# Hybrid decoder trunk on one core: x is also loaded channel-major, and the first projections multiply it before it is normed

## The chip, the core and the metric

The kernel runs on one core of a Trainium2 chip. The core has a matrix engine (PE, its weight loads PEld), a vector engine (DVE), a scalar engine (ACT), a third elementwise engine (POOL) and a queue that issues most of the transfers (SP). Each engine takes its instructions in program order; they meet through semaphores only. The metric is the device time of one execution in microseconds (us). A KB here is 1024 bytes.

## What is computed

One decoder layer for 512 tokens of 1024 channels. Cut to what matters here:

```python
h = rmsnorm(x, g_pre)              # x * rsqrt(mean(x*x, -1) + 1e-6) * g_pre
u = h @ W_in                       # 1024 x 11352, split by columns into
(gq, gk, gv, ga, gz, dq, dk, dv, iq, ik, iw, dz, xq, xz, gates) = split_cols(u)
y_gla = gla_mixer(gq, gk, gv, ga, gz, ...)     # gated linear attention, 4 heads
y_dsa = dsa_mixer(dq, dk, dv, iq, ik, iw, dz)  # indexer picks keys, then attention
y_mem = cross_mixer(xq, xz, rmsnorm(mem, g_mem), w_mem_kv)
merged = (sigmoid(g0) * (y_gla @ w_gla_out) + sigmoid(g1) * (y_dsa @ w_dsa_out)
          + sigmoid(g2) * (y_mem @ w_x_out))
x = x + rmsnorm(merged @ W_o, g_post)
```

The norm's factor rsqrt(...) belongs to a token, g_pre to a channel. So h @ W is also (x * g_pre) @ W with each token's result multiplied by its factor.

## The kernel before

Each fp32 operand is held as two parts, a high one (ACT, `high`, line 95) and the rest (DVE, `low`, lines 99 and 101), and each product is three products: high by high, high by low, low by high (`mm3`, lines 108 to 110). The weights come in chunks of 128 columns by 1024 channels: SP loads a pair of chunks (1 MB, `wraw`, two buffers), ACT makes `whi`, DVE makes `wlo`, four buffers of each.

The work is a list of units, one per chunk: 24 matmuls of 512 (or 384, in `iq`) columns for channel-major results (`unit_t`), or 48 of 256 for token-major ones (`unit_n`, used by `dv` and `gv`). A unit fills one PSUM bank with the tag `mm`, of which there are two, so a unit starts when the results of the unit two places ahead of it have been read. Bank tags `at` (three), `tp` (two) and `ac` (one) serve the small products. The main loop goes through the units; each has four quarters, and side work hangs in slots behind a quarter (`at(name, slot, function)`; a slot number above 3 counts on into the next units). Weight splits come about two units ahead of their use (`need`). Whatever is written first goes first on each engine's queue: the order is that of the code.

The units before `gqk0.0` are `dv.0`, `dv.1` (values of the sparse attention), `pc` (one chunk that holds ik, ga and iw), `gv0.0`, `gv0.1` (first values of the linear attention), `iq0.0` to `iq1.1` (indexer queries). `pc` gives `alow` (the gate's low rank part and the indexer's weights), `ar` (the operand of the gate products `pla`) and `ikh`, `ikl` (indexer keys). From `alow` PE transposes the weights `iw` (`turn_iw`, tile `iwps`); four `pla` products, one per head (`gate_log`), go on through Abs, Exp, Ln and a running sum (`gate_ln`, `gate_sum`, tile `cum`) to the factors of the linear attention (`gla_exps`). `bias_rows` makes one small product `prel`. The scores (`score`, tile `pis`) begin in `gqk0.0`.

The opening before `dv`: x is loaded token-major in eight pieces; ACT squares them, DVE and POOL make the factor, DVE scales by it and by g_pre (which PE has spread over the partitions, tile `gps`), PE transposes the result in 32 steps of 128 x 128 (tile `xps`), ACT and DVE split it into `hh` and `hl`, which all later projections read. Tokens 0 to 255 go first, `dv.0` runs on them, then tokens 256 to 511.

Of the kernel before, what the change touches and what calls it, by code (L numbers as in the profile page):

```python
# [57 lines left out]
def trunk(ctx, tc, x, mem, w_in, w_c, w_kv, w_out, w_o, cols, g_pre, g_mem, g_post, w_up, rel, onehot, out):  # L58
# [134 lines left out]
    def unit_n(name, first, lhs, tiles, done):  # L193
# [3 lines left out]
        def quarter(q):  # L197
# [3 lines left out]
            if name[:2] == "dv":  # L201
                j, half = divmod(q, 2)
                co = o[0][:, 256 * j:256 * j + 256]
                wh, wl = chunks[first + half][3]
                for p in range(3):
                    for k in range(4):
                        ah, al = lhs(4 * half + k, tiles[j])
                        pe.matmul(co, al if p == 1 else ah, (wl if p == 2 else wh)[:, :, k],  # L208
                                  start=half + p + k == 0, stop=(half, p, k) == (1, 2, 3))
                return  # L210
# [819 lines left out]
    xts = [[k2("yh", f"x{tt}{i}") for i in range(2)] for tt in range(4)]  # L1030
    xns = [[k2("acc", f"xn{tt}{i}") for i in range(2)] for tt in range(4)]

    def load_x(tt):
        for i in range(2):
            sp.dma_start(xts[tt][i], x[128 * tt:128 * tt + 128, 512 * i:512 * i + 512])
# [152 lines left out]
```

## Time and profile before

| | |
|---|---|
| median of 3 runs | 839.51 us (838.93 to 840.6) |
| profiled execution, its own time | 840.41 us |
| its span in the profile | 838.7 us |
| PE busy in the span | 825.1 us, 98% |
| DVE, ACT busy | 471.6 us (56%), 329.1 us (39%) |
| moved by DMA | 86.93 MB, mean 104 GB/s |

The page gives averages over the whole span. The profile's other views cut it by time (stretches, timeline), by engine, and by what a waiting engine waited for. Instructions of one engine overlap a little at their edges, so the distance between starts tells what one costs in a row, and a busy PE is not a PE at full rate: the distance between starts tells that too.

### The profile page before, as it was taken

The page shows a single profiled execution, that of the slowest core. Times are in us where ns is not written, and L with a number is a line of the kernel's source. Part 1 is how long each engine was busy: PE and PEld are TensorE (multiplying, and loading weights), DVE is VectorE, ACT ScalarE, POOL GpSimd, SP SyncE. Part 2 cuts the span into 40 slices and gives each one's busy share as a digit, 9 for nine tenths or more (in the row PEclk, how much of TensorE's full clock was granted, in tenths as well). Part 3 has the DMA queues.
Part 4 walks back from the last instruction along what each step waited for, and adds up shares of the span by engine and source line. Part 5 has one row for each costly group of instructions (what it writes and reads, how often), then busy time and mean ns, then how long its engine had stood idle before and what let it go on. Part 6 is the DMA issues. An engine that isn't in the chain of part 4 may idle for free.

```text
span 838.7 us, 10810 instructions
## 1 busy us (share of the span) xinstructions
PE 825.1 (98%) x4340; PEld 707.8 (84%) x4340; DVE 471.6 (56%) x839; ACT 329.1 (39%) x597; POOL 51.8 (6%) x77
## 2 busy tenths in 40 slices
PE   7999999999999999999999999999999999999997
PEld 5898888989888888888887888889989898888885
DVE  5578667777676545546677543445645554343623
ACT  5585555353433223334444422434334343322320
POOL 2000101000000020031122000000000000000000
PEclk9999999999999999999999999999999999999999
DMA  7333115221222222223122124232223241226402
GB/s 234 117 113 127 50 51 189 89 101 51 101 96 105 101 82 95 84 104 115 50 82 95 51 101 167 103 107 101 101 101 127 75 151 60 92 100 223 154 1 100
DMA packets 17101, 86.93 MB, mean 104 GB/s; under 512 B 2097, under 2 KB 2609, under 8 KB 8474
## 3 DMA queue, kind: packets, MB, share of 16 engines
q1 hardware_dynamic: 16474, 85.18, 29.1%
q10 hardware_dynamic: 576, 1.05, 0.3%
q8 instruction: 34, 0.56, 0.3%
q14 instruction: 17, 0.14, 0.1%
HBM read 83.03 MB, written 4.74 MB: 105 GB/s over the span
## 4 chain that ended last, share of the span: by engine, by line
PE 93%; DVE 2%; ACT 1%; issue 1%; DMA 1%; POOL 0%; SPq 0%; DVEq 0%; POOLq 0%; ACTq 0%
PE out L110 5%; PE out L108 5%; PE out L109 5%; PE pfin L110 2%; PE pfin L108 2%; PE pfin L109 2%; PE tpp L698 1%; PE dv.0_227 L208 1%; DMA x<-x 1%; PE dv.1_319 L208 1%; PE xps L294 1%; PE pov L109 1%; PE pa L560 1%; PE pov L110 1%; DVE wlo L99 1%
## 5 line engine op out<-in xcount | busy, mean ns | idle before, releaser
L99 DVE TENSOR_TENSOR wlo<-wraw,whi 128x1024 fp32r<-128x1024 f32 x133 | 166.0, 1249 | 78.2 <-ACT whi L95 77.4
L95 ACT ACTIVATE whi<-wraw 128x1024 fp32r<-128x1024 f32 x133 | 138.7, 1052 | 22.0 <-PE out L109 19.8
L108 PE MATMUL out<-yh,whi 128*128 128x512 f32 x192 | 75.3, 392 | 0.0
L110 PE MATMUL out<-yh,wlo 128*128 128x512 f32 x192 | 74.8, 390 | 0.0
L109 PE MATMUL out<-yl,whi 128*128 128x512 f32 x192 | 74.8, 389 | 0.0
L684 ACT ACTIVATE bm<-bm,nm 128x128 f32<-128x128 f32 (+3 forms) x32 | 18.0, 564 | 76.5 <-DVE nm L682 76.5
L668 POOL TENSOR_TENSOR bm<-toe,madd 128x128 f32<-128x128 f32 (+3 forms) x32 | 31.5, 1003 | 195.9 <-DMA toe<-bd 125.8
L110 PEld LDWEIGHTS out<-yh,wlo 128*128 128x128 f32 x192 | 36.0, 188 | 7.6
L108 PEld LDWEIGHTS out<-yh,whi 128*128 128x128 f32 x192 | 36.1, 188 | 7.3
L109 PEld LDWEIGHTS out<-yl,whi 128*128 128x128 f32 x192 | 36.1, 188 | 7.2
L273 POOL TENSOR_TENSOR rstd<-var,mhalf 128x1 f32<-128x1 f32 x10 | 5.5, 554 | 388.1 <-DVE var L929 289.7
L95 ACT ACTIVATE yh<-th 128x512 fp32r<-128x512 f32 x16 | 10.1, 632 | 46.5 <-DVE th L632 27.6
L492 DVE SCALAR_TENSOR_TENSOR gth<-gth,out 128x512 f32<-128x512 f32 x16 | 11.0, 687 | 28.1 <-PE out L110 28.1
L433 DVE MATCH_REPLACE8 madd<-m,madd 128x256 f32<-128x256 f32 (+2 forms) x48 | 25.6, 543 | 0.0
L429 DVE MAX8 m<-madd 128x8 f32<-128x256 f32 (+2 forms) x48 | 23.6, 547 | 0.0
L682 DVE CUSTOM_DVE_ANT_0 bm<-lg,bm 128x128 f32<-128x128 f32 (+3 forms) x32 | 15.5, 486 | 12.8 <-PE lg L110 12.5
L728 DVE TENSOR_TENSOR ydsa<-pov,th 128x128 f32<-128x128 f32 x32 | 7.8, 285 | 22.3 <-PE pov L110 22.3
L95 ACT ACTIVATE pth<-tpp 128x128 fp32r<-128x128 f32 (+3 forms) x32 | 13.7, 428 | 12.7 <-PE tpp L698 12.6
L99 DVE TENSOR_TENSOR yl<-th,yh 128x512 fp32r<-128x512 f32 x16 | 11.1, 693 | 11.2 <-ACT yh L95 11.2
L419 DVE SCALAR_TENSOR_TENSOR madd<-relu,iw,madd 128x256 f32<-128x256 f32 (+2 forms) x21 | 12.9, 616 | 7.6 <-ACT relu L415 7.1
L926 ACT ACTIVATE sq<-pfin 128x512 f32<-128x512 f32 x8 | 4.8, 598 | 31.2 <-PE pfin L110 31.2
L99 DVE TENSOR_TENSOR ptl<-tpp,pth 128x128 fp32r<-128x128 f32 (+3 forms) x32 | 15.4, 483 | 0.0
(1026 smaller groups left out, 2357.2 us busy)
## 6 DMA issues: line engine op xcount, KB each, us to landing
wraw<-w_in SPq DMA_DIRECT2D x43, 1024.0 KB, 4.7
wraw<-w_out SPq DMA_DIRECT2D x12, 1024.0 KB, 4.7
wraw<-w_kv SPq DMA_DIRECT2D x8, 1024.0 KB, 4.7
wraw<-w_o SPq DMA_DIRECT2D x4, 1024.0 KB, 4.8
bd<-bs SPq DMA_DIRECT2D x1, 2560.0 KB
x<-x SPq DMA_DIRECT2D x8, 256.0 KB, 6.3
toe<-bd SPq DMA_DIRECT2D x8, 256.0 KB, 4.9
xres<-x SPq DMA_DIRECT2D x4, 512.0 KB, 8.0
```

The source lines that it names most:

```text
L95: act.activation(hi, src, AF.Copy, scale=scale)
L99: dve.tensor_tensor(lo, src, f(hi), op=OP.subtract)
L108: pe.matmul(o, lh, rh, start=first, stop=False)
L109: pe.matmul(o, lh, rl, start=False, stop=False)
L110: pe.matmul(o, ll, rh, start=False, stop=last)
L208: pe.matmul(co, al if p == 1 else ah, (wl if p == 2 else wh)[:, :, k], start=half + p + k == 0, stop=(half, p, k) == (1, 2, 3))
L419: dve.scalar_tensor_tensor(sc, r[:, :n], iw[:, b, h:h + 1], sc, op0=OP.mult, op1=OP.add)
L429: dve.max(out=M8[b], in_=maskadd[b])
L433: dve.match_replace(out=maskadd[b], in_to_replace=M8[b], in_values=maskadd[b], imm_value=-FMAX)
L668: pool.tensor_tensor(bm[:, :n], Q[hp]["toe"][i][:, 384 - 128 * qb:512], maskadd[qb], op=OP.add)
L682: dve.tensor_tensor_reduce(out=bm[:, :n], in0=lg[:, :n], in1=bm[:, :n], scale=-1.0, scalar=FMAX, op0=OP.add, op1=OP.min, accum_out=nm)
L684: act.activation(bm[:, :n], bm[:, :n], AF.Exp, scale=-1.0, bias=nm, accum_out=su)
```

## The change

x comes a second time, as `x_t`, channel-major (128 partitions, 8 channel groups of 512 tokens), loaded in four pieces `xt` between the two halves of the `dv` weights; the token-major x follows behind the `gv0` weights and serves for the squares alone. ACT and DVE split `xt` times g_pre into `gh`, `gl`. The units `dv`, `gv0`, `pc` and `iq0` multiply these, and their results are scaled by the token's factor: token-major ones by a column while they are split, channel-major ones by a row that PE spreads over the partitions (`rstd_row`, tile `rps`), in a multiplication on DVE (`pc_done`, `iq_done`). The normed `hh`, `hl` are made on DVE and ACT from `xt`, the column g_pre and that row (`h_norm`, one channel group per slot), for `iq1` and all later units. There are no transposes of x and no `gps`. Twelve products on zeros stand ahead of `dv`. `dv` runs as two halves over channels in four banks. `pc` moves behind `gv0`; what hangs on it (`gate_operands`, `turn_iw`, `gate_log`, `gate_ln`, `gate_sum`, `bias_rows`) moves by some units, and `col` is issued by ACT.

```diff
-    dvh, dvl = kv4("dvh", [4, 256], F32R), kv4("dvl", [4, 256], F32R)
-    def dv_done(i, p):
-        p3 = p.rearrange("p (t d) -> p t d", t=2)
-        split(dvh[:, 2 * i:2 * i + 2], dvl[:, 2 * i:2 * i + 2], p3)
-    win_n("dv", dv_done)
+    def dv_done(tt, p):
+        if tt == 0:
+            R["dvh"], R["dvl"] = kv4("dvh", [4, 256], F32R), kv4("dvl", [4, 256], F32R)
+        split(R["dvh"][:, tt], R["dvl"][:, tt], p[:, :256], R["rstd"][:, tt:tt + 1])
+    win_n("dv", None)
+    def dv_half(half, po):
+        wh, wl = chunks[half][3]
+        for p, ks in ((0, (0, 1)), (0, (2, 3)), (1, (0, 1, 2, 3)), (2, (0, 1, 2, 3))):
+            for k in ks:
+                for tt in range(4):
+                    ah, al = g_lhs(4 * half + k, tt)
+                    pe.matmul(po[tt][:, :256], al if p == 1 else ah, (wl if p == 2 else wh)[:, :, k],
+                              start=half + p + k == 0, stop=(half, p, k) == (1, 2, 3))
+    def rstd_row():
+        p = psum("tp", "rps")
+        for tt in range(4):
+            pe.matmul(p[:, 128 * tt:128 * tt + 128], R["rstd"][:, tt:tt + 1].to_broadcast([128, 128]),
+                      ident, start=True, stop=True)
+        R["row"] = w2("row")
+        act.activation(R["row"], p, AF.Copy)
+    def h_norm(k):
+        if k < KT:
+            xt = R["xt"][k // 2][:, k % 2]
+            dve.scalar_tensor_tensor(xt, xt, gpre[:, k:k + 1], R["row"], op0=OP.mult, op1=OP.mult)
+        if k:
+            split(hh[:, k - 1], hl[:, k - 1], R["xt"][(k - 1) // 2][:, (k - 1) % 2])
-    def pc_done(p):
+    def pc_done(o):
+        p = w2("pc")
+        dve.tensor_tensor(p, o, R["row"], op=OP.mult)
...
-    add_chunks(w_c, False, 1)
-    unit_t("pc", h_rhs, pc_done)
...
+        if h == 0:
+            for j in range(2):
+                tt = 2 * i + j
+                split(vh[:, tt], vl[:, tt], p[:, 256 * j:256 * j + 256], R["rstd"][:, tt:tt + 1])
+            return
...
-    win_n("gv0", lambda i, p: gv_done(0, i, p))
+    win_n("gv0", lambda i, p: gv_done(0, i, p), g_lhs)
+    add_chunks(w_c, False, 1)
+    unit_t("pc", g_rhs, pc_done)
...
-    at("gv0.0", 0, gate_operands)
-    at("gv0.0", 2, turn_iw)
-    for h in range(4):
-        at("gv0.1", h, gate_log, h)
+    at("gv0.0", 1, rstd_row)
+    for tt in range(4):
+        at("pc", tt // 2, lambda tt=tt: dv_done(tt, R["dvps"][tt]))
+    for k in range(9):
+        at("gv0.0", 3 + k, h_norm, k)
...
-    def iq_done(i, p):
+    def iq_done(u, i, o):
+        if u == 0:
+            p = w2("iqf", n=384)
+            dve.tensor_tensor(p, o[:, :384], R["row"][:, 128:512], op=OP.mult)
...
-    at("iq0.0", 2, gate_ln, 0)
-    at("iq0.0", 3, gate_ln, 1)
+    at("iq0.0", 0, gate_operands)
+    at("iq0.0", 2, turn_iw)
+    for h in range(4):
+        at("iq0.1", h, gate_log, h)
+    at("iq1.0", 0, gate_ln, 0)
+    at("iq1.0", 1, gate_ln, 1)
...
-        at("iq0.1", 1 + 4 * h, gate_sum, h)
+        at("iq1.0", 2 + 2 * h, gate_sum, h)
...
-    at("gv0.0", 1, bias_rows)
+    at("iq0.0", 3, bias_load)
+    at("iq1.1", 1, bias_rows)
...
-        load_x(0)
-        load_x(1)
-        load_next(2)
-        load_x(2)
-        load_x(3)
...
+        for half in range(2):
+            sp.dma_start(wdv[:, half], loads[0][0][:, half])
+            for k in (2 * half, 2 * half + 1):
+                sp.dma_start(R["xt"][k], x_t[:, 2 * k:2 * k + 2])
         load_next()
+        for tt in range(4):
+            sp.dma_start(xs[tt], x[128 * tt:128 * tt + 128])
...
+        idle = psum("ac", "idle")
+        for i in range(12):
+            pe.matmul(idle, zeros[:, 0:128], zeros, start=True, stop=True)
+        R["dvps"] = [psum(t, "dvps") for t in ("at", "at", "at", "ac")]
+        for half in range(2):
+            need(half, True)
+            for k in range(4 * half, 4 * half + 4):
+                gh.append(k2("yh", f"gh{k}", F32R))
+                gl.append(k2("acc", f"gl{k}", F32R))
+                split(gh[k], gl[k], R["xt"][k // 2][:, k % 2], gpre[:, k:k + 1])
+            dv_half(half, R["dvps"])
+        need(3, True)
+        ss, v = s8("ss", 4), s8("var", 4)
+        for tt in range(4):
+            act.activation(xs[tt], xs[tt], AF.Square, scale=1.0 / 32, accum_out=ss[:, tt:tt + 1])
...
+        dve.tensor_scalar(v, ss, EPS, None, op0=OP.add)
+        R["rstd"] = const.tile([128, 4], F32, name="rstd")
+        pool.tensor_tensor(R["rstd"], v, mhalf[:, :4], op=OP.pow)
```

The code's order decides what stands where on each queue. Three places follow. On DVE, from the results of `dv` to those of `pc`, before:

```order
L99 TENSOR_TENSOR dvl<-dv.1_319,dvh 128x512
L99 TENSOR_TENSOR wlo<-wraw,whi 128x1024
L99 TENSOR_TENSOR ikl<-pc,ikh 64x512
L99 TENSOR_TENSOR wlo<-wraw,whi 128x1024
L99 TENSOR_TENSOR ar<-alow,at__432 16x512
L99 TENSOR_TENSOR uph<-upraw,at__432 16x512
```

and the last third of the same stretch after, ahead of the multiplication of `pc` by the row:

```order
L101 SCALAR_TENSOR_TENSOR dvl<-dvps,rstd,dvh 128x256 x2
L330 SCALAR_TENSOR_TENSOR xt_114<-xt_114,col,row 128x512
L99 TENSOR_TENSOR hl<-xt_113,hh 128x512
L99 TENSOR_TENSOR wlo<-wraw,whi 128x1024
L330 SCALAR_TENSOR_TENSOR xt_114<-xt_114,col,row 128x512
L99 TENSOR_TENSOR hl<-xt_114,hh 128x512
L337 TENSOR_TENSOR pc<-pc,row 128x512
L99 TENSOR_TENSOR ikl<-pc,ikh 64x512
L99 TENSOR_TENSOR hl<-xt_114,hh 128x512
```

Between the `vl` of `gv0.0` and `pc<-pc,row` there now stand eight scalings of `xt`, seven `hl`, two `wlo`, two more `vl` and four `dvl`, where DVE had nothing of its own to do for `pc` but `ikl`. On PE, the transposes `iwps` before, inside `gv0.0`, with a quarter of `gv0.0` behind them:

```order
L108 MATMUL gv0.0_418<-whi,hh 128x256
L109 MATMUL gv0.0_418<-wlo,hh 128x256
L110 MATMUL gv0.0_418<-whi,hl 128x256
L338 MATMUL iwps<-ident,alow 128x64 x4
```

and after, inside `iq0.0`, with the first `pla` behind a quarter of `iq0.0` and one of `iq0.1`:

```order
L110 MATMUL iq0.0_518<-gh_236,wlo 128x384
L364 MATMUL iwps<-ident,alow 128x64 x4
L108 MATMUL iq0.0_518<-gh_240,whi 128x384
L109 MATMUL iq0.0_518<-gl_241,whi 128x384
L110 MATMUL iq0.0_518<-gh_240,wlo 128x384
```

`iwps` has moved from a place three quarters of a `gv` unit behind `pc` to one three quarters of an `iq` unit behind it, and `pla` with it. On ACT, from the first queries `iqe` on, before:

```order
L373 ACT_TABLE_LOAD
L373 ACTIVATE ebig<-ebig 128x1024
L95 ACTIVATE iqe<-iq0.0_576 64x384
L95 ACTIVATE iqo<-iq0.0_576 64x384
L373 ACTIVATE ebig<-ebig 128x1024
L95 ACTIVATE whi<-wraw 128x1024
```

and after, up to the queries of `iq1.0`:

```order
L95 ACTIVATE iqe<-iqf 64x384
L95 ACTIVATE iqo<-iqf 64x384
L395 ACTIVATE ebig<-pla,col 128x512
L398 ACTIVATE ebig<-ebig 128x512
L404 ACT_TABLE_LOAD
L404 ACTIVATE ebig<-ebig 128x1024
L95 ACTIVATE whi<-wraw 128x1024
L404 ACTIVATE ebig<-ebig 128x1024
L95 ACTIVATE iqe<-iq1.0_641 64x384
L95 ACTIVATE iqo<-iq1.0_641 64x384
```

Abs, Exp, the table load and Ln now stand between the queries of `iq0.1` and those of `iq1.0`; before, all four heads had them done around the queries of `iq0.0`.

## Rows read from the trace of the kernel before

**Rows 1.** The page, part 1: busy us (share of the span) xinstructions.

```profile
PE 825.1 (98%) x4340; PEld 707.8 (84%) x4340; DVE 471.6 (56%) x839; ACT 329.1 (39%) x597; POOL 51.8 (6%) x77
```

**Rows 2.** Waits of PE after the opening (100 to 839): us, times, longest.

```profile
PE pov L109 <- DVE ptl L99: 1.7, 2, 1.4
```

**Rows 3.** The chain that ended last, in order of time: start, us, what.

```profile
13.28 7.61 PE dv.0_227 L208 x48
...
22.64 5.75 PE dv.1_319 L208 x48
28.39 0.23 PE pc L108
...
36.72 1.17 PE prel L449 x4
...
39.52 0.39 PE iwps L338 x4
...
42.98 0.23 PE pla L362
44.65 0.23 PE pla L362
...
64.89 0.23 PE gqk0.0_743 L108
...
79.45 0.42 PE pa L560 x2
```

**Rows 4.** Stretches: length, busy us of PE, PEld, DVE, ACT, POOL; granted clock, DMA.

```profile
60.00:70.00 10.00, 10.00 (x53) 9.10 (x52) 9.71 (x14) 6.63 (x10) 0.00 (x0) 1.00 0.59 188
70.00:80.00 10.00, 10.00 (x53) 8.30 (x51) 8.85 (x17) 5.20 (x12) 0.00 (x0) 1.00 0.34 117
200.00:400.00 200.00, 200.00 (x978) 167.87 (x975) 114.08 (x238) 68.66 (x124) 18.32 (x22) 1.00 0.26 93
```

**Rows 5.** Timeline, ACT, opening: start, us, instruction, [idle before <- releaser].

```profile
8.92 0.63 ACT L279 ACTIVATE xn<-x 128x512 f32<-128x512 f32 x1 [1.85 <-DMA x<-x]
...
11.88 1.06 ACT L95 ACTIVATE whi<-wraw 128x1024 fp32r<-128x1024 f32 x1 [0.21 <-DMA wraw<-w_in]
```

**Rows 6.** Timeline, PE, inside dv.0: groups of four matmuls of 256 columns.

```profile
16.50 1.04 PE L208 MATMUL dv.0_227<-whi,hl 128*128 128x256 f32 x4
17.35 0.67 PE L208 MATMUL dv.0_227<-wlo,hh 128*128 128x256 f32 x4
...
18.32 0.64 PE L208 MATMUL dv.0_227<-whi,hl 128*128 128x256 f32 x4
18.80 0.64 PE L208 MATMUL dv.0_227<-wlo,hh 128*128 128x256 f32 x4
```

**Rows 7.** Timeline, DVE: two or more in a row, or one.

```profile
10.51 1.41 DVE L287 SCALAR_TENSOR_TENSOR xn<-x,rstd,gps 128x512 f32<-128x512 f32 x2 [0.68 <-POOL rstd L273]
...
13.03 2.35 DVE L99 TENSOR_TENSOR wlo<-wraw,whi 128x1024 fp32r<-128x1024 f32 x2
...
22.00 2.48 DVE L99 TENSOR_TENSOR hl<-xps,hh 128x512 fp32r<-128x512 f32 x4 [1.13 <-ACT hh L95]
...
56.00 1.22 DVE L379 TENSOR_TENSOR_SCAN cum<-rmask,la_m 128x512 f32<-128x512 f32 x1
...
95.65 0.47 DVE L591 SCALAR_TENSOR_TENSOR S<-S,pd,kv 128x256 f32<-128x256 f32 x1
```

**Rows 8.** Timeline, ACT, 36 to 65.

```profile
36.32 1.28 ACT L95 ACTIVATE uph<-upraw 16x512 fp32r<-16x512 f32 x2
...
50.84 1.28 ACT L373 ACT_TABLE_LOAD   x1
...
53.10 0.47 ACT L95 ACTIVATE iqe<-iq0.0_576 64x384 fp32r<-64x384 f32 x1
...
60.77 0.48 ACT L95 ACTIVATE iqe<-iq1.0_659 64x384 fp32r<-64x384 f32 x1 [2.09 <-PE iq1.0_659 L110]
...
64.93 0.48 ACT L95 ACTIVATE iqe<-iq1.1_700 64x384 fp32r<-64x384 f32 x1 [2.09 <-PE iq1.1_700 L110]
```

More of the change, by code (lines that the diff above doesn't have):

```diff
@@ L57, in trunk @@
 @with_exitstack
-def trunk(ctx, tc, x, mem, w_in, w_c, w_kv, w_out, w_o, cols, g_pre, g_mem, g_post, w_up, rel, onehot, out):
+def trunk(ctx, tc, x, x_t, mem, w_in, w_c, w_kv, w_out, w_o, cols, g_mem, g_post, w_up, rel, onehot, out):
     nc = tc.nc
@@ L97, in low @@
     def low(lo, src, hi, scale=1.0):
-        if scale == 1.0:
+        if isinstance(scale, float) and scale == 1.0:
             dve.tensor_tensor(lo, src, f(hi), op=OP.subtract)
@@ L200, in quarter @@
             n = len(tiles)
[L201 to L210, printed above, removed]
             for i in range(2 * n * q, 2 * n * q + 2 * n):
@@ L228, in h_lhs, with g_rhs, g_lhs @@
         return hh[:, k, t], hl[:, k, t]
+    gh, gl = [], []
+    def g_rhs(k):
+        return gh[k], gl[k]
+    def g_lhs(k, tt):
+        t = slice(128 * tt, 128 * tt + 128)
+        return gh[k][:, t], gl[k][:, t]
     def win_t(name, done, **kw):
@@ L233, in win_t, with win_n @@
             unit_t(f"{name}.{i}", kw.get("rhs", h_rhs), lambda p, i=i: done(i, p), kw.get("n", T))
-    def win_n(name, done):
+    def win_n(name, done, lhs=h_lhs):
         add_chunks(w_in[PIDX[name]], True)
@@ L238, in win_n @@
         for i in range(2):
-            unit_n(f"{name}.{i}", first, h_lhs, (2 * i, 2 * i + 1), lambda p, i=i: done(i, p))
+            unit_n(f"{name}.{i}", first, lhs, (2 * i, 2 * i + 1), lambda p, i=i: done(i, p))
     ident = const.tile([128, 128], F32)
@@ L247, in trunk @@
     pool.memset(mhalf, -0.5)
-    ones1 = const.tile([1, 128], F32)
-    dve.memset(ones1, 1.0)
+    zeros = w2("zeros", F32R)
+    dve.memset(f(zeros), 0.0)
     rmask = k2("yl", "rmask")
@@ L267, in trunk @@
                        fill=-1e30, base=0, channel_multiplier=1)
-    col = const.tile([128, 6], F32)
-    ba, ggla = col[:, 0:4], col[:, 4:6]
+    col = const.tile([128, 14], F32)
+    ba, ggla, gpre = col[:, 0:4], col[:, 4:6], col[:, 6:14]
     def rstd_of(v, n):
@@ L380, in gate_sum @@
         cum.append(c)
-    at("pc", 3, lambda: None)
-    at("gv0.0", 0, gate_operands)
-    at("gv0.0", 2, turn_iw)
-    for h in range(4):
-        at("gv0.1", h, gate_log, h)
-    iqs = []
-    def iq_done(i, p):
-        ev, od = k2("acc", "iqe", F32R, 384), k2("acc", "iqo", F32R, 384)
-        high(ev[0:64], p[0:64, :384])
-        high(od[64:128], p[64:128, :384])
+    at("gv0.0", 1, rstd_row)
[3 more added lines that the diff above has]
+        at("gv0.0", 3 + k, h_norm, k)
+    iqs = []
+    def iq_done(u, i, o):
+        if u == 0:
+            p = w2("iqf", n=384)
+            dve.tensor_tensor(p, o[:, :384], R["row"][:, 128:512], op=OP.mult)
+            tag = ("yl", None)[i]
+        else:
+            p, tag = o[:, :384], "acc"
+        ev, od = [k2(tag, n, F32R, 384) if tag else w2(n, F32R, 384) for n in ("iqe", "iqo")]
+        high(ev[0:64], p[0:64])
+        high(od[64:128], p[64:128])
         l = w2("iql", F32R, 384)
-        low(l[0:64], p[0:64, :384], ev[0:64])
-        low(l[64:128], p[64:128, :384], od[64:128])
+        low(l[0:64], p[0:64], ev[0:64])
+        low(l[64:128], p[64:128], od[64:128])
         sp.dma_start(f(ev[64:128]), f(l[0:64]))
@@ L723, in dsa_out @@
         for kb in range(qb + 1):
-            mm3(po[:, :256], dvh[:, kb, dsl], dvl[:, kb, dsl],
+            mm3(po[:, :256], R["dvh"][:, kb, dsl], R["dvl"][:, kb, dsl],
                 pth[:, kb].rearrange("p h q -> p (h q)"),
@@ L1027, in trunk @@
         at(f"fin0{i}", 1, split_b, i)
[L1030 to L1035, printed above, removed]
-    with tc.manual_schedule():
-        grow = w4("grow")
-        sp.dma_start(grow[0:1], g_pre)
-        load_x(0)
-        load_x(1)
-        load_next(2)
-        load_x(2)
-        load_x(3)
+    with tc.manual_schedule():
+        R["xt"] = [kv4(f"xt{k}", [2, 512], F32) for k in range(4)]
+        xs = [w4(f"x{tt}") for tt in range(4)]
+        act.dma_start(col, cols)
+        wdv = wp.tile([128, 2, 1024], F32, name="wraw", tag="wraw", bufs=2)
+        loads[0][2] = wdv
+        state["load"] = 1
+        for half in range(2):
+            sp.dma_start(wdv[:, half], loads[0][0][:, half])
+            for k in (2 * half, 2 * half + 1):
+                sp.dma_start(R["xt"][k], x_t[:, 2 * k:2 * k + 2])
         load_next()
-        sp.dma_start(col, cols)
+        for tt in range(4):
+            sp.dma_start(xs[tt], x[128 * tt:128 * tt + 128])
         R["upraw"] = w2("upraw")
@@ L1140, in _layout @@
     a["x"] = np.ascontiguousarray(np.asarray(inputs["x"])[0])
+    a["x_t"] = np.ascontiguousarray(a["x"].T.reshape(KT, 128, T).transpose(1, 0, 2))
     a["mem"] = np.ascontiguousarray(np.asarray(inputs["mem"])[0])
```

57 lines of the change are left out of this document (13 added, 44 removed).

## The prediction, made before the changed kernel ran

> **What bounds the kernel now.** I read the page's busy times first, then the chain, then the waits of TensorE (PE), then stretches and single rows. PE is busy 98% of the span [rows 1] and, after the opening, waits 1.7 us in all [rows 2]: whatever shortens or lengthens PE's queue shows in the end time almost whole. The first unit that both kernels share unchanged is gqk0.0; it starts at 64.89 [rows 3]. So the question is when gqk0.0 starts in the changed kernel and whether PE waits after that. The other engines look idle on average (DVE 56%, ACT 39%), but not in the stretch that the change loads: DVE is busy 9.71 of 10 us at 60 to 70 and 8.85 at 70 to 80, against 114 of 200 later [rows 4]. That is the row I trust most.
>
> **The change, part by part. The opening.** Loads land in the order of SP's queue. Before, the fourth 256 KB (1 MB in all) release their reader at 8.92 and the second half of the dv weights (2 MB in all) at 11.88 [rows 5]: 1.48 us per 512 KB. The new order is dv weights, two pieces of x_t, dv weights, two pieces, 1 MB of gv0 weights, four tiles of x. So the first x_t piece (1 MB in all) lands at 8.92, then 10.40, 11.88, 13.36, 14.84, gv0 at 17.8, the last x tile at 23.7. The first split (0.63) lets PE start dv at 9.55, against 13.28 now. dv is 24 groups of four products of 256 columns. A group starts 0.85 after the last one at the lower rate and 0.48 at the higher [rows 6], which are 1.2 and 2.4 GHz for 4 x 256 columns (the granted clock reads 1.00 in both stretches); before, dv began low at 13.28 and rose at 17.35, 4.1 us on. Low for 4.1 us gives an end at 22.9; high throughout gives 21.7, since the pieces hold PE up until 11.6 anyway. The 12 products on zeros (512 columns, so 0.43 at the lower rate, 5.1 us) stand ahead of the data and are free; whether they bring the clock up no row tells. I take 22.4 and keep both ends. Before, dv ended at 28.39 [rows 3]. Gone with it: the transposes, 1.75 us on the path for the last 16 (dv.0 ends at 20.89, dv.1 starts at 22.64), and of the lower rate's loss, 7.61 - 5.75 = 1.9 [rows 3], all or half.
>
> **gv0.0 and the row of scales.** A quarter of gv takes 44.65 - 42.98 - 0.23 = 1.44 [rows 3]. Half of gv0.0 ends at 25.3. Then PE multiplies rstd by the identity: it needs the last square (23.7 + 1.06, as a 1024-wide ACT row [rows 5]) and two one-column steps on DVE and POOL, which with the read of the sum now take from 9.55, the end of the square [rows 5], to 10.51, the scaling [rows 7], 0.96: 25.75, so PE waits 0.45. Four fp32 products at 0.21 (pa, [rows 3]) add 0.84. gv0.0 ends at G = 29.45.
>
> **DVE's queue, the term that decides.** From G, PE has gv0.1 (5.76), pc (24 x 0.23 = 5.52) and three quarters of iq0.0 (3 x 1.04; a unit is 64.93 - 60.77 = 4.16 [rows 8]): it reaches the transposes iwps at G + 14.4. They read alow, a copy of the scaled pc, and that scaling is DVE's. Ahead of it in DVE's queue, all behind the vl of gv0.0: two vl pairs that alternate with ACT (1.8 and 1.4), 8 scalings of xt (0.70 each), 7 hl (0.62), 2 wlo (1.17), 4 dvl (0.47 as S) [rows 7], pc itself 0.62: 1.8 + 1.4 + 5.6 + 4.3 + 2.3 + 1.9 + 0.6 = 18.0. With ar and alow on ACT (0.64 each, as uph [rows 8]) alow is there at A = G + 19.3 = 48.75. **PE waits 4.9.** Before, the same scaling did not exist: ACT read pc from its bank at once. Queued behind the waiting iwps is all of PE; nobody covers it.
>
> **The next waits follow from the same two queues.** Steps that no row shows go by their width: 512 wide 0.64 on ACT and 0.62 (two tensors) or 0.70 (with a scalar) on DVE, 384 wide 0.47 on ACT and 0.56 on DVE, 1024 wide 1.06 and 1.17. After A: iwps 0.39 and two quarters, PE wants the first gate product pla at A + 2.5. It needs uph, behind ikh, hh, at_, two uph, at_ on ACT and one DVE step: 0.64 + 0.64 + 0.64 + 1.28 + 0.64 + 0.62 = 4.45. Wait 1.95; P = 53.2. The fourth pla wants a third bank at P + 3.8; it is free after wlo, iqf, iqe, iqo, one Abs and la_m, P + 4.5. Wait 0.7. Then iq1.0 and iq1.1 with prel (4.16 + 4.16 + 1.17): P + 14.2. gqk0.0 takes the bank of iq1.0, which DVE's iql frees. That stands behind, in turn, from P + 3.8: Exp 0.64, whi 1.06, Abs 0.64, la_m 0.70, wlo 1.17, la_m 0.70, iqf 0.56, iqe and iqo 0.94, Abs and Exp 1.28, a table load 1.28, Ln 1.06, whi 1.06, wlo 1.17, subtraction 0.62, cum 1.22, two iql 1.12, 15.2 in all [rows 7, 8]: P + 19.0. **Wait 4.8**; gqk0.0 starts at Q = 72.2, 7.3 later than now. Last, the backlog delays the first two relu: from Q, DVE has three subtractions with scans (5.5), a wlo, two iql and et, 8.5 us, then ACT has et, whi and relu (2.1), so the first is done at Q + 10.6, where PE wants its bank at Q + 8.9 (wait 1.6). The second, behind wlo, qd, q, q2h, costs 1.5 more. By 90 DVE has caught up; the 200 to 400 row leaves it idle for 43% and I add nothing there.
>
> **Edits at no cost.** w_c and the iq0 weights are issued later on SP (SP waits for x tiles to land), yet land near 25 to 30 and are wanted after 32; if x came 5 us late this cover is gone. The one-hot load and prel move to iq1.1: their reader is the spread in gz1.0, far later. The second x read (2 MB) is in the landings above. ar's copy to its other rows is issued once ar is there and has the 4.45 to land.
>
> **Sum.** Without any wait PE would reach gqk0.0 at G + 30.4 (5.76 + 5.52 + 4 x 4.16 + 0.39 + 4 x 0.23 + 1.17 [rows 3]) = 59.85, a gain of 5.0. Waits after G: 4.9 + 1.95 + 0.7 + 4.8 + 3.1 = 15.45. Net +10.5. The profiled execution (span 838.7, time 840.41) becomes 850.9; it lies 0.9 above the median of the runs, 839.51, so the median becomes **850.0**.
>
> **Rivals.** *PE is not held (faster).* Busy shares say DVE and ACT have room: then only the opening counts, 839.5 - 5.0 = 834.5. It decides if DVE's 18.0 shrinks below 14.4 - 1.3 = 13.1 and the later 15.2 below 10.4. Against it: nearly every one of those durations is a row, queues go in order, and DVE is already full at 60 to 70. The page Perfetto Trace Analysis of the Trainium skill (Identifying the Most-Contended Engine) would side with this rival: it says to improve the engine with the highest occupancy first, and that is PE here. Rows 4 speak against it for this stretch. Chance 0.06. *Half held:* waits of about 5 instead of 15.5 leave the time where it is, 839.5. Chance 0.04.
> *The clock falls in the waits.* Two waits are near 5 us, longer than any of the kernel now after its opening. Rows 6 show a PE that ran at half rate after an opening with pauses. Each fall would cost about what the opening's did, 1.9 [rows 3]. One fall gives 852, two 854. The page TensorE: Matmul & The Clock Gate (HAM oscillation) says that idle gaps put the array back to half rate; no row here shows one falling. Chance 0.20.
> *The loads are late.* The row of scales needs 6 MB to have landed, twice what came before dv now. At 2 us later than the rate above the rps product waits and all slides: 852. Chance 0.08.
> My forecast has the rest, 0.62.
>
> **How the numbers follow.** Around 850.0: the clock at the start moves it -0.7 to +0.6, the landings by about 1 either way, 256-wide steps at 0.40 instead of 0.47 and no alternation -1.5: low end 846.5. Two falls, or one with late loads, set the high end at 855.5; it leaves out the two rivals that are not slower. A run of this kernel can tell 0.2% (1.7 us) from no change. Faster 0.06, same 0.04, slower 0.90.
>
> **What would show it.** Right: dv starting near 9.5 and gv0.0 ending near 29; waits of PE at iwps for ACT's alow of 4 to 5 us, at pla for DVE, and ahead of gqk0.0 for iql; DVE busy over 9 of 10 us at 30 to 48 where it now idles; gqk0.0 at 70 to 74. Wrong: gqk0.0 before 65, or iwps without a wait, which would mean that DVE's steps from SBUF are shorter than those rows, or that the vl of gv0.0 do not hold the scalings back. A dv that starts after 12 would put the miss on the loads.

## The result and the profile after

The changed kernel takes 849.31 us (median of 4 runs, 849.21 to 849.48), the kernel before 839.34 us beside it: a ratio of 1.0116, 95% interval 1.0099 to 1.0134. The prediction said 850.0 with a range of 846.5 to 855.5, and slower with a chance of 0.90. The span of the profiled execution grew from 838.7 to 847.5, by 8.8, and the median by 10.0: the profiled execution of the kernel before was one of its longer ones.

Part 1 of the page answers [rows 1]: PE does no more work, it stands longer.

```profile
PE 826.0 (97%) x4324; PEld 708.0 (84%) x4324; DVE 479.0 (57%) x851; ACT 335.3 (40%) x602; POOL 50.5 (6%) x74
```

The waits of PE from 0 to 100 (what waited, for whom, us, times, longest); after 100 there is nothing to set beside [rows 2]:

```profile
PE iwps L364 <- ACT alow L341: 4.9, 1, 4.9
PE gqk0.0_738 L108 <- DVE iql L99: 4.2, 1, 4.2
...
PE pis L458 <- ACT relu L461: 0.6, 1, 0.6
PE pa L610 <- ACT relu L461: 0.5, 1, 0.5
...
```

PE's timeline at the points that the prediction steps through (start, us, instruction, idle before and its releaser):

```profile
8.04 2.60 PE L315 MATMUL dvps<-whi,gh 128*128 128x256 f32 x16 [1.25 <-ACT gh L95]
...
26.71 0.28 PE L108 MATMUL gv0.1_385<-whi,gh 128*128 128x256 f32 x1
...
40.91 0.34 PE L110 MATMUL iq0.0_518<-gh,wlo 128*128 128x384 f32 x1
46.12 0.69 PE L364 MATMUL iwps<-ident,alow 64*128 64x64 f32 x4 [4.88 <-ACT alow L341]
...
50.74 0.45 PE L393 MATMUL pla<-ar,uph 128*128 128x512 f32 x1
...
55.32 0.50 PE L393 MATMUL pla<-ar,uph 128*128 128x512 f32 x1 [0.50 <-DVE la_m L397]
...
69.81 0.77 PE L108 MATMUL gqk0.0_738<-hh,whi 128*128 128x512 f32 x1 [4.17 <-DVE iql L99]
70.37 0.63 PE L109 MATMUL gqk0.0_738<-hl,whi 128*128 128x512 f32 x1
70.80 0.63 PE L110 MATMUL gqk0.0_738<-hh,wlo 128*128 128x512 f32 x1
```

The opening is faster than forecast, then PE loses all of that and more, most of it in and right behind two waits. What it waits for at the first is at the end of DVE's queue, and behind that of ACT's. DVE's timeline from 43 and ACT's from 44:

```profile
43.61 0.68 DVE L99 TENSOR_TENSOR hl<-xt,hh 128x512 fp32r<-128x512 f32 x1
44.21 0.68 DVE L337 TENSOR_TENSOR pc<-pc,row 128x512 f32<-128x512 f32 x1
```

```profile
44.93 0.62 ACT L95 ACTIVATE ar<-pc 16x512 fp32r<-16x512 f32 x1 [2.97 <-DVE pc L337]
45.46 0.61 ACT L341 ACTIVATE alow<-pc 64x512 f32<-64x512 f32 x1
```

The last matmul of pc ends at 38.1; its scaling starts at 44.21, and DVE worked without a pause from 36.3 until then. The stretches show the clock as well (busy us and instructions of PE, PEld, DVE, ACT, POOL; then granted clock, DMA share, GB/s):

```profile
40.00:45.00 5.00, 1.25 (x8) 0.92 (x6) 4.89 (x8) 0.70 (x2) 0.00 (x0) 0.90 0.16 28
45.00:50.00 5.00, 3.88 (x14) 3.76 (x15) 2.09 (x4) 4.85 (x9) 0.00 (x0) 0.50 0.68 243
...
65.00:70.00 5.00, 0.83 (x5) 0.54 (x4) 4.36 (x6) 4.93 (x9) 0.00 (x0) 0.79 0.00 0
70.00:75.00 5.00, 5.00 (x13) 3.90 (x14) 4.90 (x6) 2.47 (x4) 0.00 (x0) 0.53 0.38 84
```

After each of the two waits the granted clock is at the lower level (0.50 of full speed, 1.2 GHz, from 46 to 50.7 and from 69.8 to 74), and the products of gqk0.0 start 0.43 apart instead of 0.23. So the prediction's rival of the falling clock did happen, twice. Whether it cost anything is the first question below. Starts of the same units in the two traces, from the timelines:

| unit | before | after | later by |
|---|---|---|---|
| iq0.0 | 48.06 | 37.94 | -10.12 |
| iq1.0 | 56.41 | 55.65 | -0.76 |
| gqk0.0 | 64.73 | 69.81 | 5.08 |
| gqk0.1 | 70.70 | 78.15 | 7.45 |
| gz0.1 | 86.95 | 96.00 | 9.05 |
| gqk2.0 | 141.67 | 150.76 | 9.09 |

(pc stands ahead of gv0 in the kernel before, so iq0.0 is the first unit that has the same units ahead of it in both; of its 10.12 us, 2.5 are iwps, prel and the four pla, 0.39 + 1.17 + 0.92, which now come later.) So the opening gained 7.6, and 16.7 were lost from there to gz0.1. From 96 on the two kernels run in step (gqk2.0 is as late as gz0.1): the whole loss is made before that.

### The profile page after: what moved, and what is told of

The parts are those of the page before. It is cut to its first block, busy times and chain, and to the rows that moved or that the text cites. A ratio compares the mean times of both kernels' runs of the same rounds, so it can differ in the third digit from the quotient of the medians.

```text
span 847.5 us, 10786 instructions
## 1 busy us (share of the span) xinstructions
PE 826.0 (97%) x4324; PEld 708.0 (84%) x4324; DVE 479.0 (57%) x851; ACT 335.3 (40%) x602; POOL 50.5 (6%) x74
## 4 chain that ended last, share of the span: by engine, by line
PE 88%; DVE 5%; ACT 3%; issue 2%; DMA 1%; POOL 0%; DVEq 0%; POOLq 0%; SPq 0%; ACTq 0%
PE out L108 5%; PE out L110 5%; PE out L109 5%; PE pfin L110 2%; PE pfin L108 1%; PE pfin L109 1%; PE dvps L315 1%; DVE wlo L99 1%; PE tpp L748 1%; DMA xt<-x_t 1%; ACT whi L95 1%; PE pa L610 1%; PE pov L109 1%; PE pov L110 1%; PE pov L108 1%
## 5 line engine op out<-in xcount | busy, mean ns | idle before, releaser
L273 POOL TENSOR_TENSOR rstd<-var,mhalf 128x1 f32<-128x1 f32 x6 | 3.3, 552 | 374.9 <-DVE var L979 289.7
```

## The experiments

My theory: DVE (and ACT behind it) sets PE's pace from the end of gv0.0 to gz0, first through the place of pc's scaling in DVE's queue, then through the chain from the gate products `pla` to the query parts `iql` of iq1.0, which must be read before gqk0.0 gets its bank. Rivals: the falls of the clock cost the time; a bank, ACT or the loads hold PE; DVE has too much to do whatever the order. All medians below are to be read beside 849.31 for the changed kernel, which did not run again, and 839.2 to 839.7 for the kernel before, which ran along each time; differences of about half a microsecond say nothing.

**e1_filled: PE kept busy in the two waits.**

```diff
+    def fill(n, s):
+        p = psum("ac", "fill")
+        for i in range(n):
+            pe.matmul(p, s[:, 0:128], s, start=True, stop=True)
+    at("iq0.0", 2, lambda: fill(20, gh[0]))
+    at("iq1.1", 3, lambda: fill(17, hh[:, 0]))
     at("iq0.0", 2, turn_iw)
```

> The changed kernel's PE waits 4.9 us ahead of iwps and 4.2 ahead of gqk0.0, and its granted clock falls to half in both and comes back only 4.6 and 4.9 us after PE has started again. Here 20 products on data at hand stand ahead of iwps and 17 ahead of gqk0.0 (512 columns each, 0.22 us at the high rate, 4.3 and 3.7 us), written to a bank that nobody reads, so that PE is busy in the waits and the clock should stay up. Theory (DVE and ACT set the pace there, so a PE at half rate loses nothing): the time stays at 849.3, within 0.7; the lost time shows as waits instead, 1.9 us at the first pla (uph is ready at 50.48, PE at 48.6) and about 3 at the first relu instead of 1.1. Rival (each fall costs what it slows, 12 products at 0.32 instead of 0.17 = 1.8 us, and 4.85 us at half rate = 2.4 us): 845.1, with gqk0.0 some 2 us earlier.

Measured 849.77 (849.46 to 850.28); in the profiled executions the mean granted clock is 0.999 instead of 0.991, and 1.00 in every stretch from 40 to 80. The waits of PE from 20 to 160:

```profile
PE pis L465 <- ACT relu L468: 2.5, 2, 1.2
PE pla L393 <- DVE uph L99: 1.8, 1, 1.8
...
PE pa L617 <- ACT relu L468: 0.5, 1, 0.5
PE iwps L364 <- ACT alow L341: 0.3, 1, 0.3
PE gqk0.0_777 L108 <- DVE iql L99: 0.3, 1, 0.3
```

The clock stayed up and nothing was gained. What the half rate took in the changed kernel stands here as waits: 1.8 for uph, and 2.5 instead of 0.6 for relu. gqk0.0 starts at 70.06, gz0.1 at 96.25. So the two falls cost nothing that a run can tell: PE ran slowly only where it would otherwise have waited.

**e2_unscaled: eight DVE steps taken out.**

```diff
     def h_norm(k):
-        if k < KT:
-            xt = R["xt"][k // 2][:, k % 2]
-            dve.scalar_tensor_tensor(xt, xt, gpre[:, k:k + 1], R["row"], op0=OP.mult, op1=OP.mult)
         if k:
             split(hh[:, k - 1], hl[:, k - 1], ...)
```

> The eight scalings of xt on DVE (0.66 to 0.74 us each, 5.3 in all) are left out, so iq1 and all later units work on x without its norm; all else is the changed kernel. Theory (iwps waits because pc's scaling stands at the end of DVE's queue): pc's scaling starts when pc ends, at about 39 instead of 44.2, alow is there about 4 us earlier, the wait at iwps falls from 4.9 to about 1, the later waits stay as they are, and the time is 845.3 (844 to 846.5). Rival (ACT, a bank or the loads hold iwps): the wait stays above 4 and the time at 849.

Measured 845.67 (845.58 to 846.71). Waits of PE from 20 to 160:

```profile
PE gqk0.0_730 L108 <- DVE iql L99: 4.2, 1, 4.2
PE pla L390 <- DVE uph L99: 1.7, 1, 1.7
PE iwps L361 <- ACT alow L338: 1.2, 1, 1.2
```

5.3 us less on DVE ahead of pc's scaling take 3.7 off the wait at iwps and 3.6 off the time; the wait ahead of gqk0.0 is the same 4.2. (That the clock did not fall in the wait at iwps made no difference, as in e1.)

**e3_pc_direct: the same work on DVE, but alow without it.**

```diff
-        p = w2("pc")
-        dve.tensor_tensor(p, o, R["row"], op=OP.mult)
+        p = o
```

> pc is not multiplied by the row; ACT reads ar, alow and ikh from pc's bank at once, as in the kernel before (the gate, the indexer's keys and weights are then without the norm). DVE keeps all its other work. Theory (the place in DVE's queue): alow no longer stands behind DVE's queue but only behind ACT's, whose last step ahead of ar is the hh that follows the seventh scaling (done at 41.2): alow is there near 43 instead of 46.1 and the wait at iwps falls from 4.9 to 1.5 to 2, the time to 846.3 (845 to 847.5). Rival (DVE's total work, wherever pc's scaling stands): nothing is gained, since DVE loses only 0.6 us of work: 848.7 or more.

Measured 846.62 (846.46 to 847.23). Waits of PE:

```profile
PE gqk0.0_736 L108 <- DVE iql L99: 4.1, 1, 4.1
PE iwps L363 <- ACT alow L340: 1.9, 1, 1.9
PE pla L392 <- DMA ar<-ar: 1.3, 1, 1.3
```

DVE has 0.6 us less to do and the kernel is 2.7 faster: it is the place in the queue that counted here. The remaining 1.9 is ACT's queue: the hh at 41.58, which waits for one of DVE's scalings, stands ahead of ar.

**e5_gz0_between: two units more between the gate products and gqk0.0.**

```diff
+    z_units("gz0")
     for h in range(4):
         win_t(f"gqk{h}", ...)
-        z_units(f"gz{h}")          # for h = 0
-    at("iq1.0", 0, gate_ln, 0)
-    at("iq1.0", 1, gate_ln, 1)
+    at("iq0.0", 13, gate_ln, 0)
+    at("iq0.0", 14, gate_ln, 1)
-        at("iq1.0", 2 + 2 * h, gate_sum, h)
+        at("iq0.0", 15 + 2 * h, gate_sum, h)
```

> The two units gz0.0 and gz0.1 (24 products of 512 columns each, 5.6 us each) stand ahead of gqk0.0 instead of behind gqk0.1, and the logarithms and sums of the gate come three units later; what hung on gz0 hangs on the units that now follow gqk0.1. Same work in all. Theory (PE comes to gqk0.0 too early for the chain Abs, Exp, Ln, split, sum on ACT and DVE): the wait of 4.2 ahead of gqk0.0 is gone, no fall of the clock there, the iwps wait stays at 4.9: 845 (843.5 to 846.5). Rival (DVE and ACT simply have too much to do between 28 and 80): the wait comes back at the mm bank of gz0.0 or at the relu, and the time stays at 848 to 849.5.

Measured 845.79 (844.71 to 845.90). (In this kernel and in e9 the top-k steps, which hang on gv1.0, begin before the last scores are in, so the last block's selection isn't the reference's; the steps are as many and as long.) Waits of PE from 20 to 300, the three longest, and PE's timeline at the start of dv:

```profile
PE iwps L364 <- ACT alow L341: 4.9, 1, 4.9
PE gv2.0_1632 L109 <- DVE wlo L99: 1.4, 1, 1.4
PE gqk2.1_1590 L108 <- DVE th L520: 0.5, 1, 0.5
```

```profile
7.95 3.54 PE L315 MATMUL dvps<-whi,gh 128*128 128x256 f32 x16 [1.77 <-ACT gh L95]
```

The wait ahead of gqk0.0 is gone and did not come back near by, at a bank or a relu; the first is untouched. So they are two waits, not one backlog. But 1.9 us of waits for DVE are new at gqk2.1 and gv2.0, 80 us later. And this execution lost 1.1 in its opening, which the edit does not touch: the granted clock reads 0.63 from 8 to 10, and gv0.0 starts at 21.16 instead of 20.07. Its time, 845.89, is near three of the four runs; the fourth took 844.71. So the 3.5 us by which the median is faster are, by these figures, rather less than the new distance is worth.

**e6_no_idle: the opening's clock.**

```diff
-        for i in range(12):
-            pe.matmul(idle, zeros[:, 0:128], zeros, start=True, stop=True)
+        pe.matmul(idle, zeros[:, 0:128], zeros, start=True, stop=True)
```

> Of the twelve products on zeros ahead of dv one is left. In the changed kernel they run from 1.50 to 6.8 at 0.44 us each, the lower rate, and dv, which starts at 8.04, takes 12.0 us for its 96 products, the higher rate from nearly its start. Theory (they bring the clock up): dv starts at 8.0 at half rate for some 4 us, as dv did in the kernel before from 13.28 to 17.35, loses about 2 us of it, ends at 22 instead of 20.1, and all behind it slides by that: 851.3 (850.5 to 852). Rival (the clock comes up by the time the data are there, or the loads and the row of scales have 2 us of slack): 849.3.

Measured 851.04 (850.07 to 851.52; the profiled execution is the longest). PE's timeline, dv:

```profile
8.04 3.78 PE L315 MATMUL dvps<-whi,gh 128*128 128x256 f32 x16 [5.74 <-ACT gh L95]
11.62 3.19 PE L315 MATMUL dvps<-whi,gl 128*128 128x256 f32 x16
```

gv0.0 starts at 22.32 instead of 20.07, and the profiled execution is 2.3 longer than that of the changed kernel. (The granted clock reads 1.00 in both; the rate is told here by the starts, 16 products in 3.58 instead of 2.43.) The same half rate that was free at 46 and 70 costs 1.7 in the medians here, where PE waits for nobody from the start of dv to iwps: even the row of scales is there in time.

**e8_small_pieces: the opening's loads.**

```diff
-                sp.dma_start(R["xt"][k], x_t[:, 2 * k:2 * k + 2])
+                for j in range(2):
+                    sp.dma_start(R["xt"][k][:, j], x_t[:, 2 * k + j])
```

> x_t is loaded in eight pieces of 256 KB (2 KB in a row) instead of four of 512 KB (4 KB in a row), the size in which the kernel before loaded x. In the kernel before the first MB released its reader at 8.92, in the changed kernel at 7.26, and the prediction had 8.92 for both. Theory (size of the pieces and their issues set the pace of the opening's loads): gh starts near 8.3, dv 1 us later than 8.04, and the whole kernel with it: 850.3 (849.8 to 851). Rival (the pace is that of the bytes, the rest was the place in the queue of g_pre and its 0.4 us of issue): gh at 7.3 to 7.6, time 849.3 to 849.6.

Measured 850.12 (850.03 to 850.36): the forecast time, by another way. ACT's timeline, the first gh and the last square:

```profile
6.41 2.67 ACT L95 ACTIVATE gh<-xt,col 128x512 fp32r<-128x512 f32 x4 [0.51 <-DMA xt<-x_t]
...
21.15 1.06 ACT L1119 ACTIVATE x<-x 128x1024 f32<-128x1024 f32 x1 [1.16 <-DMA x<-x]
```

Small pieces let the first one be used earlier (gh at 6.41 instead of 7.26, dv at 7.18), not later, so their size is not what made the first loads of the kernel before slow. The last x tile comes at 21.15 instead of 20.32, and PE, which is earlier, waits 1.3 for the row of scales. My mechanism was wrong; that the sum came out was luck.

**e7_pool: the scalings on POOL.**

```diff
-            dve.scalar_tensor_tensor(xt, xt, gpre[:, k:k + 1], R["row"], op0=OP.mult, op1=OP.mult)
+        pool.tensor_tensor(xt, xt, R["row"], op=OP.mult)
...
+        split(hh[:, k], hl[:, k], R["xt"][k // 2][:, k % 2], gpre[:, k:k + 1])
```

> The eight multiplications of xt by the row go to POOL (a tensor by tensor product of 128 by 512; its sum of that shape in the attention takes 1.57 us, so 12.6 in all, from 24.7 to 37.3), g_pre goes into the split (a scale on ACT, a scalar on DVE, 0.06 us more each). DVE loses 5.3 us of work ahead of pc's scaling, as when the scalings were left out (845.67), but the results stay those of the reference. Theory (only DVE's queue held PE): wait at iwps 1 to 1.5, time 845.5 (844.5 to 846.5). Rival (POOL and DVE hold each other up when both work out of SBUF, or POOL is too slow and iq1 waits for hh): DVE's steps in 25 to 40 get longer than 0.69 and the time is 847.5 or more.

Measured 850.45 (850.06 to 850.84), 1.1 slower than the changed kernel. POOL's timeline, and DVE's beside it:

```profile
24.93 12.65 POOL L329 TENSOR_TENSOR xt<-xt,row 128x512 f32<-128x512 f32 x8 [1.92 <-ACT row L325]
```

```profile
28.74 0.48 DVE L101 SCALAR_TENSOR_TENSOR vl<-gv0.0_322,rstd,vh 128x256 fp32r<-128x256 f32 x1 [0.54 <-ACT vh L95]
29.35 4.85 DVE L101 SCALAR_TENSOR_TENSOR hl<-xt,col,hh 128x512 fp32r<-128x512 f32 x3
34.12 2.30 DVE L99 TENSOR_TENSOR wlo<-wraw,whi 128x1024 fp32r<-128x1024 f32 x1
36.35 1.78 DVE L101 SCALAR_TENSOR_TENSOR hl<-xt,col,hh 128x512 fp32r<-128x512 f32 x1
...
39.68 0.75 DVE L101 SCALAR_TENSOR_TENSOR hl<-xt,col,hh 128x512 fp32r<-128x512 f32 x1
```

While POOL works (to 37.6), hl takes 1.6 to 1.8 instead of 0.75 and wlo 2.30 instead of 1.22; vl (28.74), one of whose tensors lies in PSUM, keeps its 0.48. POOL is slowed too: its steps start 1.25 apart from 26.44 to 30.20 and 1.70 apart from there to 35.31, beside DVE's hl. The 5.3 us taken off DVE came back as longer steps. The wait at iwps is 4.7, and one of 1.3 ahead of iq0.0, for vl, is new.

**e9_three_parts: POOL, uph ahead of time, gz0 between.** The diffs of e7 and e5, and the uph half of `gate_operands` moved to the third quarter of gv0.0.

> Three parts together: the multiplications of xt by the row on POOL; uph split ahead of time (behind the row, when ACT and DVE idle) instead of between alow and the first pla; gz0.0 and gz0.1 ahead of gqk0.0 with the logarithms and sums three units later. Theory (three separate waits, each taken away where it comes from): iwps wait 1 to 1.5 instead of 4.9, none at pla above 0.5, none ahead of gqk0.0, the clock at its high level after the opening: 849.3 - 3.6 - 0.5 - 4.2 - 2.4 (half rate and the relu behind it), 838.6 (836.5 to 840.5), level with the kernel before at 839.4. Rival (what is taken from one place comes back at the next, since DVE has 10 us more to do in the same stretch): 842 or more, with new waits at the mm banks or relu between 60 and 110.

Measured 845.20 (844.72 to 845.38). Waits of PE:

```profile
PE iwps L367 <- ACT alow L341: 4.7, 1, 4.7
PE iq0.0_523 L108 <- DVE vl L101: 1.5, 1, 1.5
```

Of the three parts gz0 did its share, with the same waits behind it as in e5 (0.6 at gqk2.1, 1.4 at gv2.0); POOL spoiled the first, as in e7, and an early uph is worth nothing while PE comes from iwps later still. The forecast of 838.6 failed on the POOL part.

**e11_pc_first and e10_pc_first_gz0: the order instead of the work.**

```diff
+    add_chunks(w_c, False, 1)
+    unit_t("pc", g_rhs, lambda p: pc_done(p))     # behind dv, ahead of gv0
     win_n("gv0", lambda i, p: gv_done(0, i, p), g_lhs)
-    add_chunks(w_c, False, 1)
-    unit_t("pc", g_rhs, pc_done)
-    at("gv0.0", 1, rstd_row)
+    at("pc", 1, rstd_row)
...
-    at("iq0.0", 0, gate_operands)
-    at("iq0.0", 2, turn_iw)
+    at("gv0.0", 0, gate_operands)     # e10: slot 1, up_split ahead of it
+    at("gv0.0", 2, turn_iw)           # e10: slot 1
```

The diff shows e11, with e10's slots beside it. In e11 `h_norm` runs from the first quarter of gv0.0 to that of iq0.0, the dv results come in the last half of gv0.1 and `gate_log` from the second quarter of iq0.0; in e10 `h_norm` runs from the third quarter of pc to the end of iq0.0, `gate_log` from the third quarter of iq0.1, and gz0 stands as in e5.

> Only the first of these two orders: pc ahead of gv0, gate operands and iwps in gv0, dv results in gv0.1, gate products from the second quarter of iq0.0 on; gz0 stays behind gqk0.1. Theory (the iwps wait goes, but the gate products now come while DVE still has h_norm and the dv results to do, and the chain to the query parts of iq1.0 is as long as it was): no wait at iwps, 4 to 6 us of waits at the pla instead, some 2 ahead of gqk0.0: 847 (845.5 to 848.5). Rival (the place of pc alone was the fault): pla without waits and 843 or less.

Measured 846.85 (846.73 to 847.99). Waits of PE:

```profile
PE pla L393 <- DVE dvl L101: 2.5, 2, 1.9
PE pla L393 <- DVE la_m L397: 2.4, 1, 2.4
PE gqk0.0_738 L108 <- DVE iql L99: 2.4, 1, 2.4
```

> Two orders changed in the changed kernel, with the work the same. pc goes back to its old place ahead of gv0 (the row of scales is spread inside pc), so that its multiplication stands ahead of DVE's other work, and what hangs on it (gate operands, uph, iwps) comes in gv0, the gate products in iq0.1; h_norm and the dv results are spread over gv0 to iq0.1. And gz0.0, gz0.1 stand ahead of gqk0.0 as in the run before, with the top-k steps eight slots later so that they follow the last scores. Theory (the order on DVE and the distance on PE made the loss, the added DVE work itself has room from 25 to 75): no wait at iwps and none ahead of gqk0.0, 849.3 - 4.9 - 4.2 - 4.0 = 836.2, and some 3 to 4 us of new short waits at pla and the mm banks: 840 (838.5 to 841.5), level with the kernel before at 839.3. Rival (DVE has 10 us more to do in this stretch and PE pays for it wherever it stands): 844 or more, the waits merely elsewhere.

Measured 840.88 (11 runs, 840.53 to 841.63), against 839.72 for the kernel before (21 runs): ratio 1.0018, interval 1.0009 to 1.0027. Waits of PE from 5 to 300, the three longest:

```profile
PE pla L396 <- DVE la_m L400: 2.0, 1, 2.0
PE gv2.0_1624 L109 <- DVE wlo L99: 1.4, 1, 1.4
PE iq1.0_630 L108 <- DVE iqf L428: 1.3, 1, 1.3
```

In e11 the wait at iwps is gone, but 4.9 of waits stand at the pla products instead and 2.4 of the 4.2 ahead of gqk0.0 are left. Alone, the order of pc is worth 2.5 and the distance 3.5; e10 is worth 8.4. No instruction of DVE was saved, so 8.4 of the 10 us by which the kernel got slower were order. That the two together are worth more than their sum is not explained by a run: e5 lost 1.1 in its opening, and e10 also splits uph early and has `h_norm` and `gate_log` in other slots than e11.

What is left has two parts. PE still waits 4.4 us for DVE in four places between 48 and 69, which takes most of the opening's gain. Even so gqk2.0 starts at 139.78, 1.9 before its start in the kernel before (141.67, the same units ahead of it); then come 0.6 at gqk2.1 and the 1.4 at gv2.0, and gv2.1 is 0.6 later than before. These two waits stand in the three kernels with gz0 in its new place (e5, e9, e10) and in none with it in the old one. So the last microsecond goes with the place of gz0, not with the stretch that the change loads. That the four earlier waits come of DVE's added work I only argue; no run took that work away and kept the order.

**e12_before_idle: the idle products alone, in the kernel before.**

```diff
+        idles(2)      # products on zeros, 512 columns, into an mm bank
         gps = [psum("at", "gps") for _ in range(2)]
...
+        idles(2)
         def h_scale(tt, ss):
...
+        idles(6)
         h_scale(1, ss[1])
```

> The kernel before with ten products on zeros (512 columns) in the gaps of its opening: two ahead of gps, two behind it, six between the first and the second set of xps. Theory (a busy PE brings the clock up, but the opening of the kernel before is paced by DVE: the last xn is done at 20.86, where dv.0 ends at 20.89): dv.0 runs at 0.48 per group of four from its start and ends near 19.0, then PE waits for the third and fourth xn, dv.1 starts 0 to 0.7 us earlier than 22.64: time 838.9 (838.3 to 839.4), no difference that can be measured. Rival (dv.0 at the low rate cost its 1.9 us in full, as the prediction counted it): 837.4.

Measured 839.16 (11 runs), 0.9993 of the kernel before, interval 0.9984 to 1.0002: no difference that can be told. PE's timeline, and below it that of the kernel before:

```profile
12.71 0.72 PE L208 MATMUL dv.0_240<-whi,hh 128*128 128x256 f32 x4
...
19.30 2.43 PE L296 MATMUL xps<-ident,xn 128*128 128x128 f32 x16
21.49 0.72 PE L208 MATMUL dv.1_332<-whi,hh 128*128 128x256 f32 x4
```

```profile
20.73 1.91 PE L294 MATMUL xps<-ident,xn 128*128 128x128 f32 x16
22.39 0.72 PE L208 MATMUL dv.1_319<-whi,hh 128*128 128x256 f32 x4
```

dv.0 started at 12.71, ran at the high rate from there and ended at 19.3, 1.4 earlier; the later starts moved by 0.9 only, because the transposes then waited for DVE's last xn (it ends at 20.96, at 20.86 in the kernel before). None of the kernels here beats the kernel before by more than a measurement can tell.

## Why the prediction was right, point by point

- **The opening was mis-sized by 2.7, in the cautious direction.** gh starts at 7.26, not 8.92; dv at 8.04, not 9.55; it ends at 20.07, not 22.4; the last x tile is used at 20.32, not 23.7; PE does not wait for the row of scales (forecast 0.45). G is 26.71, not 29.45. Two terms failed. The landings were carried over from [rows 5] as a rate, 1.48 per 512 KB; here 5 MB more take from 7.26 to 20.32, 1.31 per 512 KB, and the first MB comes 1.7 earlier. e8 shows that the size of the pieces is not the reason; what held the loads of the kernel before back stays open. And the rate of dv: I took the middle of two ends, and e6 shows it was the high end, thanks to the idle products.
- **DVE's queue to pc was right.** Forecast 18.0 from G to the end of pc's scaling, measured 44.89 - 26.71 = 18.2, and it holds by its parts: 2.2 and 1.4 for the vl pairs (forecast 1.8 and 1.4), 5.6 for the scalings (5.6), 4.4 for hl (4.3), 2.3 for wlo (2.3), 1.6 for dvl (1.9), 0.7 for pc (0.6); alow at G + 19.3, measured G + 19.36; the wait 4.9, measured 4.88. e2 and e3 show that it is that queue.
- **The wait at the first pla (1.95) is not in the trace, and is still right:** PE at half rate arrives at 50.74, when uph is ready (DVE's last step on it runs from 49.88 to 50.56). With the clock up, in e1, it is 1.76. The fourth pla waited 0.50 (forecast 0.7).
- **The wait ahead of gqk0.0:** forecast 4.8 and Q = P + 19.0; measured 4.17 and 69.81 - 50.74 = 19.07. From G to Q the forecast was 42.75, the trace has 43.10.
- **After Q:** forecast 3.1 as two relu waits, measured 9.09 - 5.08 = 4.0. Here the form differs: 2.4 at half rate in gqk0.0 (8.34 instead of 5.97), 0.6 for relu and 0.5 at pa, which I had not listed. In e1 the 4.0 are waits (2.5 for relu, 0.5 at pa, the rest spread). "DVE has caught up by 90" holds to 96.
- **The sum:** -2.7 in the opening, +0.35 to Q, +0.9 behind it give 10.5 - 1.5 = 9.0 against 8.8 in the span. The 0.7 between 850.0 and 849.31 is thus smaller than the terms' own errors; the opening's error and the late term's partly cancel, which is luck. So is the last step: the forecast for the profiled execution was 850.9 against 849.21, and taking off 0.9, the distance of the kernel before's profiled execution from its median, hid 1.0 of those 1.7, though the changed kernel's lies only 0.1 from its own.
- **The rival of the clock was told apart wrongly.** It had 0.20, with 1.9 a fall. Two falls came. The Trainium skill's page TensorE: Matmul & The Clock Gate (HAM oscillation) says this of idle gaps, and the trace agrees with 0.50 after each. But e1 puts their price at nothing (849.77 with the clock up). The price of 1.9 was read off the length of dv.0 in the kernel before, and e12 shows that it was not the price there either: at the high rate dv.0 ended 1.4 earlier and all behind it started only 0.9 earlier, since DVE's xn came no sooner. So the 1.9 that the prediction lists as gone with the old opening was too much as well; its sum did not use it. Only in e6, where PE waits for nobody from the start of dv to iwps, does the half rate cost about that (1.7). The rival should have been priced where it would fall.
- **The rival of late loads and both rivals that were not slower did not come.** For the rival in which PE is not held the price was 834.5. The Trainium skill's page Perfetto Trace Analysis (Identifying the Most-Contended Engine), taken over the whole span, would have PE, the busiest engine, as the one to relieve; the trace does not agree for this stretch: PE got 7.6 us earlier through the opening, and 16.7 were lost behind it.

## What to carry to other kernels

An engine that is half idle on average can set the pace where a change puts its new work: write down that stretch's queues in order and add the rows up, as was done for DVE here to 0.2 us. When results are scaled after a product instead of the operand ahead of it, each scaling becomes a wait for every reader of the result, so put it ahead of the bulk work on that queue, and leave enough other work between it and its readers. A rate that fell, or a step that got early, is worth what it moves in the slowest chain there, which may be nothing.

## What the runs showed of the hardware

- POOL and DVE slow each other when both work out of SBUF (e7): beside POOL's multiplication of two tiles, DVE's steps with both tensors in SBUF took about twice as long (hl 1.6 to 1.8 instead of 0.75, wlo 2.30 instead of 1.22), those with one tensor in PSUM the same (vl 0.48); POOL's steps of 128 x 512 started 1.70 apart beside hl and 1.25 apart just before. The Trainium skill's page GPSIMD Engine Reference (Specifications) names this: POOL's SBUF interfaces are shared with VectorE, with contention for DVE instructions that have two SBUF inputs. The trace agrees, and gives the price.
- After standing idle for 4.9 and 4.2 us PE was at the lower clock when it came back, and reached the higher one 4.6 and 4.9 us later (granted clock 0.50 until 50.7 and 74.7).
- Twelve products on zeros from 1.5 to 6.8 were enough for dv to run at the higher rate from about its start at 8.04, and one product was not (e6). Twelve were not always enough: in e5's profiled execution they ended at 6.18, PE stood idle for 1.77 us before dv instead of 1.25, and the granted clock read 0.63 from 8 to 10.
